# State-space input in one pass over the input blocks, values' projection in another PSUM bank, attention scores one tile earlier

## The chip, the cores and the metric

The kernel runs on one core of a Trainium2 chip. The core has a matrix engine (TensorE, PE in the profile, with its weight loads as PEld), VectorE (DVE), ScalarE (ACT), GpSimd (POOL) and SyncE (SP), which issues most DMAs. Matmul results go to PSUM: eight banks of 128 x 512 fp32. Everything else lies in SBUF. The metric is the device time of one execution in microseconds; the kernel before is given by the median of three runs.

## The reference

One decoder layer on 512 tokens of width 1024, all in fp32:

```
x = x + 1/2 SwiGLU(RMSNorm(x))
u = RMSNorm(x)
u_ssm, q, k, v, xq, g_ssm, g_attn, g_mem = split(u @ w_in)
branch 1: S5 state-space model on u_ssm (32 groups of 16 channels, 64 states each), GELU, GLU
branch 2: causal dilated attention, 3 patterns x 4 heads of 64, mixed by their softmax denominators
branch 3: cross attention (4 heads of 128) to 256 memory tokens
x = x + (sum over branches of sigmoid(gate) * branch) @ w_out
x = x + 1/2 SwiGLU(RMSNorm(x));  out = RMSNorm(x)
```

The output must agree with the fp32 reference, so almost every product is made of three fast matmuls: each operand is split into a rounded high part and the remainder (`wh`, `wl` for weights, `uh`, `ul` for the normalised input), and high x high, high x low and low x high are added up in PSUM.

## The kernel before

Activations stand transposed, as eight tiles of 128 features x 512 tokens. The input `u` of the middle part is held as `U`: eight pairs `uh[k]`, `ul[k]`. A weight chunk is 1024 x 256 (`load_chunk`, two buffers `wraw`); `split` (L120 to L126) makes its halves on ScalarE (L124) and VectorE (L125), three buffers each. `block_T` (L643) multiplies one 128-column half of a chunk with all of U: 8 blocks x 3 matmuls (L133, L134, L135) into one PSUM bank, 128 x 512.

In order of the program:

- Feed-forward 1 ends with the norm of x. `ffn1` (L632 to L638) then forms U block by block: VectorE makes `u` (L637), ScalarE `uh`, VectorE `ul` (L143, L144). While that goes on, TensorE works on keys and values of the memory tokens (`mem_kv`).
- The PSUM pool `ps_b` is opened for the middle part: two banks `mm` for projections, three `sc`, two `s1`, one `acc`.
- `ssm_in` (L652): four tiles of the state-space input, one after the other through `block_T` and the two `mm` banks. Each is copied to SBUF (`ub`, two buffers, L659) and written to a scratch in DRAM (`hd`, from ScalarE's queue, L661). `ssm_units` later reads it back in another layout (`stk`, on SP's queue, L676) and begins with matmuls into `s1` (L690).
- A loop over three chunks projects q, k and v. `split_q` and `split_k` (first chunk) copy a bank out in four and six pieces on ScalarE and VectorE (L930 to L942). `nat_rows` (L811) makes the values token by token: four row tiles of 128 x 256, two to a bank, 24 matmuls each (L822 to L824), again in the two `mm` banks. After each projection `tick` advances the state-space work.
- Cross attention, with its gates, uses `sc` and `s1`.
- Attention (L1003 to L1035): two pairs of heads x four row tiles, d = 0 to 7. `attn_tile` (L853) makes for two heads the scores (`sc` and `s1`: L862, L870), adds the bias and takes the maximum on VectorE (L874, L876), does the softmax (ScalarE L767, VectorE L769, L770), transposes the probabilities on TensorE (twelve, L883, through `sc` banks, copied out by ScalarE, L884) and multiplies with v into the bank `acc` (L890). After each tile come, for the same d, the state-space gate (24 matmuls) and the gated product of the state-space output (`pb`, `pa`, 12 matmuls each). After four tiles `acc` is split into `ath`, `atl`, the input of the attention's up-projection in the next stage.

The program's order is not the order on an engine. A planner takes each engine's instructions by priority, which follows the order of emission with a few shifts (`cur_priority`, `high_priority`), as soon as its own timing model calls them ready, and lays down a fixed order per engine. A tile of a pool gets its buffer or bank in that planning too. On the chip each engine then works strictly in its order and waits where an input or a buffer is late.

Of the kernel before, what the change touches and what calls it, by code (L numbers as in the profile page):

```python
# [20 lines left out]
P = 128  # L21
# [63 lines left out]
def kernel(ctx, tc, x, mem, ffn1_norm, ffn1_w_in, ffn1_w_down, mix_norm, w_in, a_re, a_im, log_dt,  # L85
# [21 lines left out]
    def load_chunk(w, k0, nk, c0, ncol):  # L107
        raw = wpool.tile([P, nk, ncol], F32, name="wraw", tag="wraw", bufs=2)
        nc.sync.dma_start(raw, w[k0 * P:(k0 + nk) * P, c0:c0 + ncol].rearrange("(k p) c -> p k c", p=P))
        return raw  # L110
# [532 lines left out]
    def block_T(raw, j):  # L643
        p = ps_tile("mm")
        mm_T(p, split(raw[:, :, j * P:(j + 1) * P]), U)
        return p
# [3 lines left out]


    def ssm_in(pool):  # L652
        hd = []
        for i in range(0, 4, 2):
            raw = load_chunk(W, 0, KD, i * P, 2 * P)
            for j in range(2):
                p = block_T(raw, j)
                b = pool.tile([P, T], F32, name="ub", tag="ub", bufs=2)
                S.activation(b, p, AF.Copy)  # L659
                d = dpool.tile([P, T], F32, name=f"hd{i + j}")  # L660
                nc.scalar.dma_start(d, b)  # L661
                hd.append(d)
        return hd

    def ssm_units(pool, hd):
# [93 lines left out]

    def softmax_rows(s, mx, pool, scale, n, tag, pr=None):  # L760

        nm = pool.tile([P, 1], F32, name=tag + "nm", tag=tag + "nm", bufs=2)
        V.tensor_scalar(nm, mx, -scale, None, op0=ALU.mult)
        sm = pool.tile([P, 1], F32, name=tag + "sm", tag=tag + "sm", bufs=2)
        if pr is None:
            pr = pool.tile([P, n], F32, name=tag + "p", tag=tag + "p", bufs=2)
        S.activation(pr, s, AF.Exp, bias=nm, scale=scale, accum_out=sm)  # L767
        ri = pool.tile([P, 1], F32, name=tag + "ri", tag=tag + "ri", bufs=2)
        V.reciprocal(ri, sm)  # L769
        V.tensor_scalar(pr, pr, ri, None, op0=ALU.mult)  # L770
        return pr
# [36 lines left out]
            for t in range(2):  # L808
                nc.scalar.dma_start(kvd[4 + 2 * t + c], mvs[t].rearrange("p a k -> p (a k)").bitcast(F32))

    def nat_rows(raw, src, nt, dst, eng=None):  # L811

        pss = [ps_tile("mm") for _ in range((nt + 1) // 2)]
        ws = [split(raw[:, kk:kk + 4, :], eng or V) for kk in range(0, KD, 4)]
        for t in range(nt):
            o = pss[t // 2][:, (t % 2) * 256:(t % 2) * 256 + 256]
            for k in range(KD):
                h, l = ws[k // 4]
                h, l = h[:, k % 4, :], l[:, k % 4, :]
                ah, al = src[k]  # L820
                ah, al = ah[:, t * P:(t + 1) * P], al[:, t * P:(t + 1) * P]
                TE.matmul(o, ah, h, start=k == 0, stop=False)  # L822
                TE.matmul(o, ah, l, start=False, stop=False)  # L823
                TE.matmul(o, al, h, start=False, stop=k == KD - 1)  # L824
        for t in range(nt):
            o = pss[t // 2][:, (t % 2) * 256:(t % 2) * 256 + 256]
            dst(t, o)
# [22 lines left out]
        return xo  # L850


    def attn_tile(pool, hp, r, qT, kT, v, bias, pacc):  # L853

        tok = slice(r * P, (r + 1) * P)
        pts = []
        heads = (2 * hp, 2 * hp + 1)
        s0 = [ps_tile("sc", 3) for _ in heads]
        s1 = [ps_tile("s1", 2) for _ in heads]
        kh, kl = kT[hp]  # L860
        for e in range(2):
            whole = TE.matmul(s0[e], qT[hp][e][:, tok], kh[e], start=True, stop=False)  # L862

        last = whole.ins
        rows = [(s0[e], qT[hp][e][halves[e], tok], kl[halves[e], :], False) for e in range(2)]
        rows += [(s1[e][:, p * P:(p + 1) * P], qT[2 * p + 2 + hp][halves[e], tok], kT[2 * p + 2 + hp][halves[e], tok], True)
                 for p in range(2) for e in range(2)]
        for o, q, k, st in rows:
            with tc.issue_after(last):
                last = TE.matmul(o, q, k, start=st, stop=True).ins  # L870
        for e, h in enumerate(heads):
            sb = pool.tile([P, 6 * P], F32, name="sb", tag="sb", bufs=3)
            mx = pool.tile([P, 2], F32, name="amx", tag="amx", bufs=3)
            V.tensor_tensor_reduce(sb[:, :T], s0[e], bias[h][:, (3 - r) * P:(7 - r) * P], scale=1.0, scalar=NEG,  # L874
                                   op0=ALU.add, op1=ALU.max, accum_out=mx[:, 0:1])
            V.tensor_tensor_reduce(sb[:, T:], s1[e][:, :256], bias[h][:, 7 * P:9 * P], scale=1.0, scalar=mx[:, 0:1],  # L876
                                   op0=ALU.add, op1=ALU.max, accum_out=mx[:, 1:2])
            pr = softmax_rows(sb, mx[:, 1:2], pool, 1.0, 6 * P, "at", pr=sb)
            pt = pool.tile([P, 6, P], F32, name="pt", tag="pt", bufs=4)
            for b0, nb in ((0, 4), (4, 2)):  # L880
                ta = ps_tile("sc", 3)
                for b in range(nb):
                    TE.transpose(ta[:, b * P:(b + 1) * P], pr[:, (b0 + b) * P:(b0 + b + 1) * P], ident)  # L883
                S.activation(pt[:, b0:b0 + nb, :], ta[:, :nb * P].rearrange("p (k q) -> p k q", k=nb), AF.Copy)  # L884
            pts.append(pt)

        for b in (4, 5, 0, 1, 2, 3):
            for e in (1, 0):
                kt, c = (b, heads[e] * 64) if b < 4 else (r, (b - 3) * 256 + heads[e] * 64)
                TE.matmul(pacc[halves[e], tok], v[kt][:, c:c + 64], pts[e][:, b, :], start=b == 4, stop=b == 3)  # L890

    def up_block(raw, j, src):
# [53 lines left out]
    for c in range(3):  # L946
        for lst, nm, base in ((qT, "q", 512), (kT, "k", 1280)):
            raw = load_chunk(W, 0, KD, base + c * 256, 256)
            for j in range(2):
                p = block_T(raw, j)  # L950
                if c == 0:
                    lst.append((split_q if nm == "q" else split_k)(p, j))
                else:
                    o = qp.tile([P, T], F32, name=f"{nm}T{2 * c + j}", tag=f"{nm}T{2 * c + j}")
                    S.activation(o, p, AF.Copy, scale=0.125 if nm == "q" else 1.0)
                    lst.append(o)
                tick()
        raw = load_chunk(W, 0, KD, 2048 + c * 256, 256)
        nat_rows(raw, U, 4, lambda t, o: V.tensor_copy(v[t][:, c * 256:(c + 1) * 256], o))
        tick()  # L960

    tick(1000)
# [40 lines left out]
    with sb_pool("att") as ap:  # L1003
        A, bias = [], []
        for h in range(4):
            bt = ap.tile([P, 9, P], F32, name=f"bias{h}")
            for g in range(4):
                src = bass.AP(tensor=brep.tensor, offset=brep.offset + h * 9 * 256 + 127 - 32 * g,
                              ap=[[NB - 1, 32], [256, 9], [1, P]])
                nc.sync.dma_start(bt[32 * g:32 * g + 32], src)  # L1010
            bias.append(bt.rearrange("p s k -> p (s k)"))
        for hp in range(2):
            pacc = ps_tile("acc", 1)
            for r in range(4):
                attn_tile(ap, hp, r, qT, kT, v, bias, pacc)
                d = 4 * hp + r
                if d not in gates:
                    ssm_gate(d)
                if d % 2 == 0:
                    rg = wpool.tile([P, 8, 2 * P], F32, name="wraw", tag="wraw", bufs=2)  # L1020
                    for s in range(2):
                        nc.sync.dma_start(rg[:, 4 * s:4 * s + 4, :],
                                          w_glu[0][:, s * D + d * P:s * D + (d + 2) * P].rearrange("(k p) c -> p k c", p=P))
                j = d % 2
                g = gates[d]
                pb = up_block(rg[:, 4:8, :], j, Y)
                t = gp.tile([P, T], F32, name="glt", tag="glt", bufs=2)
                S.activation(t, pb, AF.Tanh, scale=0.25)
                pa = up_block(rg[:, 0:4, :], j, Y)
                V.scalar_tensor_tensor(t, t, 1.0, pa, op0=ALU.add, op1=ALU.mult)  # L1030
                V.scalar_tensor_tensor(t, g, 1.0, t, op0=ALU.add, op1=ALU.mult)
                V.scalar_tensor_tensor(merged[d], t, 0.25, merged[d], op0=ALU.mult, op1=ALU.add)
            A.append((qp.tile([P, T], F32R, name=f"ath{hp}", tag=f"qs{hp}0"),
                      qp.tile([P, T], F32R, name=f"atl{hp}", tag=f"qs{hp}1")))
            split_plain(pacc, *A[-1])  # L1035
# [280 lines left out]
```

## Time and profile before

| | |
|---|---|
| Median of 3 runs | 1258.8 us (1258.47 to 1259.54) |
| The profiled execution | 1257.0 us, its span 1255.2 us |
| TensorE busy | 1232.7 us, 98% |
| VectorE, ScalarE, GpSimd busy | 793.4, 468.1, 102.6 us |
| Granted TensorE clock, mean | 0.997 |
| State-space input, first to last matmul | 413.4 to 438.5 us |
| First values' projection begins | 465.7 us |
| Attention, first transposes to last values | 686.0 to 798.2 us |

A row of the timeline gives start, duration, engine, line of the kernel, operation, output <- inputs, shape, count, and in brackets the idle time of the engine before it with what ended it. A row of the waits gives the waiting engine and line, what it waited for, us in total, times, longest. A row of the windows gives the stretch, its length, the busy time of each engine with its instructions, the granted clock, the DMA engines' share and GB/s (with a filter to one engine, only that one). A row of the groups gives line, engine, operation, tensors, shapes, count, busy us, mean ns, and idle time before with its releasers. Starts of matmuls overlap: one begins before its predecessor has drained, so the step from start to start is the rate.

### The profile page before, as it was taken

The numbers are of one execution on the slowest core, as the hardware profiler recorded it, in microseconds if no ns is written. First come the engines' busy times: TensorE is split into PE (matmuls) and PEld (weight loads), VectorE is DVE, ScalarE is ACT, GpSimd is POOL, SyncE is SP. The second block draws the span as 40 slices with busy tenths as digits, with TensorE's granted clock in tenths as the row PEclk, the third lists the DMA queues.
The fourth block names the chain that finished last, engine by engine and source line by source line (L and its number), as shares of the span: only waits on it lengthen the run. The fifth ranks groups of instructions, "written<-read, shape, count | busy, mean of one in ns | idle before, by whom it ended". The sixth has DMA issues, their size and how long they took to land.

```text
span 1255.2 us, 17065 instructions
## 1 busy us (share of the span) xinstructions
PE 1232.7 (98%) x6692; PEld 1046.6 (83%) x6692; DVE 793.4 (63%) x1514; ACT 468.1 (37%) x731; POOL 102.6 (8%) x83
## 2 busy tenths in 40 slices
PE   7999999999999999999999999899999999999997
PEld 6888888788889789998878777788888899899896
DVE  7999456876547567644535555455498557657664
ACT  4322232233324433234433444334245445345343
POOL 3000000000003033330000000001200001001002
PEclk9999999999999999999999999999999999999999
DMA  6233323754218844653118222234625457457411
GB/s 204 86 113 117 135 95 100 186 172 148 93 61 270 253 144 145 193 163 104 51 34 193 67 68 76 67 110 139 184 80 167 103 150 183 125 149 181 123 64 67
DMA packets 165767, 162.01 MB, mean 129 GB/s; under 512 B 28180, under 2 KB 149076, under 8 KB 165396
## 3 DMA queue, kind: packets, MB, share of 16 engines
q1 hardware_dynamic: 133488, 137.68, 35.1%
q0 software_dynamic: 8576, 8.65, 4.7%
q10 hardware_dynamic: 23624, 14.61, 3.9%
q8 instruction: 52, 0.85, 0.3%
q14 instruction: 27, 0.22, 0.1%
HBM read 145.94 MB, written 16.16 MB: 129 GB/s over the span
## 4 chain that ended last, share of the span: by engine, by line
PE 94%; DVE 3%; DMA 1%; ACT 1%; issue 0%; SPq 0%; ACTq 0%
PE ps_mm L133 21%; PE ps_mm L134 20%; PE ps_mm L135 20%; PE ps_mm L1160 4%; PE ps_mm L1161 4%; PE ps_mm L1158 4%; PE ps_mm L1216 3%; PE ps_mm L1217 3%; PE ps_mm L1218 3%; PE ps_mm L822 1%; PE ps_mm L824 1%; PE ps_mm L823 1%; PE ps_sc L883 1%; DMA wraw<-in_ffn_w_in_dram 1%; PE ps_sc L733 1%; PE ps_acc L890 1%
## 5 line engine op out<-in xcount | busy, mean ns | idle before, releaser
L124 ACT ACTIVATE wh<-wraw 128x1024 fp32r<-128x1024 f32 (+2 forms) x226 | 211.5, 938 | 470.3 <-PE ps_mm L134 330.5
L125 DVE TENSOR_TENSOR wl<-wraw,wh 128x1024 fp32r<-128x1024 f32 (+2 forms) x226 | 248.6, 1102 | 141.2 <-ACT wh L124 140.6
L133 PE MATMUL ps_mm<-uh,wh 128*128 128x512 f32 x768 | 301.8, 393 | 0.8 <-ACT uh L143 0.6
L134 PE MATMUL ps_mm<-ul,wh 128*128 128x512 f32 x768 | 300.4, 391 | 1.8 <-DVE ul L144 1.8
L135 PE MATMUL ps_mm<-uh,wl 128*128 128x512 f32 x768 | 299.9, 391 | 0.0
L134 PEld LDWEIGHTS ps_mm<-ul,wh 128*128 128x128 f32 x768 | 144.3, 188 | 32.8 <-DVE ul L144 2.8
L133 PEld LDWEIGHTS ps_mm<-uh,wh 128*128 128x128 f32 x768 | 144.3, 188 | 32.1 <-ACT uh L143 1.0
L135 PEld LDWEIGHTS ps_mm<-uh,wl 128*128 128x128 f32 x768 | 144.2, 188 | 29.9
L217 POOL TENSOR_TENSOR sqacc<-sqacc,sqk 128x512 f32<-128x512 f32 x12 | 20.2, 1682 | 686.1 <-ACT sqk L216 686.0
L134 PE MATMUL ps_mm<-gl,wh 128*128 128x512 f32 x176 | 70.0, 398 | 0.0
L133 PE MATMUL ps_mm<-gh,wh 128*128 128x512 f32 x176 | 69.9, 399 | 0.0
L135 PE MATMUL ps_mm<-gh,wl 128*128 128x512 f32 x176 | 69.8, 398 | 0.0
L1217 PE MATMUL ps_mm<-wl,gh 128*128 128x512 f32 x176 | 69.4, 394 | 0.0
L1218 PE MATMUL ps_mm<-wh,gl 128*128 128x512 f32 x176 | 69.1, 394 | 0.0
L1216 PE MATMUL ps_mm<-wh,gh 128*128 128x512 f32 x176 | 67.6, 395 | 0.0
L125 DVE TENSOR_TENSOR wl<-s,wh 128x1024 fp32r<-128x1024 f32 x32 | 39.2, 1224 | 42.8 <-ACT wh L124 42.8
L124 ACT ACTIVATE wh<-s 128x1024 fp32r<-128x1024 f32 x32 | 33.9, 1061 | 61.7 <-PE ps_mm L1218 26.1
L143 ACT ACTIVATE gh<-ff_t 128x512 fp32r<-128x512 f32 x44 | 27.1, 627 | 52.6 <-DVE ff_t L315 33.6
L135 PEld LDWEIGHTS ps_mm<-gh,wl 128*128 128x128 f32 x176 | 33.0, 188 | 8.2 <-issue 0.2
L133 PEld LDWEIGHTS ps_mm<-gh,wh 128*128 128x128 f32 x176 | 33.0, 188 | 8.2 <-issue 0.2
L1218 PEld LDWEIGHTS ps_mm<-wh,gl 128*128 128x128 f32 x176 | 33.2, 188 | 7.7
L1217 PEld LDWEIGHTS ps_mm<-wl,gh 128*128 128x128 f32 x176 | 33.2, 188 | 7.5
(395 smaller groups left out, 2388.8 us busy)
## 6 DMA issues: line engine op xcount, KB each, us to landing
wraw<-in_ffn_w_in_dram SPq DMA_DIRECT2D x34, 1024.0 KB, 5.2
wraw<-in_w_in_dram SPq DMA_DIRECT2D x25, 1024.0 KB, 5.4
wraw<-in_ffn_w_down_dram SPq DMA_DIRECT2D x12, 768.0 KB, 4.4
s<-in_ffn_w_in_dram SPq DMA_DIRECT2D x16, 512.0 KB, 3.7
s<-in_ffn_w_in_dram POOLq DMA_DIRECT2D x16, 512.0 KB, 6.2
wraw<-in_ffn_w_down_dram SPq DMA_DIRECT2D x8, 1024.0 KB, 5.2
wraw<-in_ffn_w_down_dram SPq DMA_DIRECT2D x10, 512.0 KB, 3.5
wraw<-in_xattn_w_kv_dram SPq DMA_DIRECT2D x4, 1024.0 KB, 8.0
```

The costliest lines, as they stand in the source:

```text
L124: S.activation(h, raw, AF.Copy)
L125: eng.tensor_tensor(l, raw, h.bitcast(F32), op=ALU.subtract)
L133: TE.matmul(ps, h[:, k, :], rhs[k][0], start=first and k == 0, stop=False)
L134: TE.matmul(ps, h[:, k, :], rhs[k][1], start=False, stop=False)
L135: TE.matmul(ps, l[:, k, :], rhs[k][0], start=False, stop=last and k == n - 1)
L143: S.activation(h, src, AF.Copy)
L1158: TE.matmul(o, h[:, k, cols], rhs[k][0], stop=False, **st)
L1160: TE.matmul(o, h[:, k, cols], rhs[k][1], stop=False, **st)
L1161: TE.matmul(o, l[:, k, cols], rhs[k][0], stop=k == 3, **st)
L1216: TE.matmul(pd[r], gh[:, tok], h, start=st, stop=False)
L1217: TE.matmul(pd[r], gh[:, tok], l, start=False, stop=False)
L1218: TE.matmul(pd[r], gl[:, tok], h, start=False, stop=en)
```

## The change

Three places are edited.

1. `ssm_in`: both weight chunks are loaded first, and four banks (two `mm`, two `s1`) are taken at once. For each block k of U the three matmuls of all four tiles are emitted, so the tiles grow together and end together. The weights are split by halves of k (blocks 0 to 3, then 4 to 7) over the whole 256 columns, instead of by column halves over all k. The copies and the writes of `hd` come after all matmuls.
2. `nat_rows` gets a flag `spare`, set for the values of the q, k, v loop: its first bank (tokens 0 to 255) is `acc`, its second `mm`.
3. `attn_tile` is cut into `attn_scores` (scores, bias, softmax) and `attn_values` (transposes, product with v). The scores of tile d + 1 are emitted before the values of tile d. The score tiles have four buffers instead of three, the small softmax columns four instead of two.

```diff
     def ssm_in(pool):
+        raws = [load_chunk(W, 0, KD, i * P, 2 * P) for i in (0, 2)]
+        ps4 = [ps_tile("mm"), ps_tile("mm"), ps_tile("s1", 2), ps_tile("s1", 2)]
+        for k0 in range(0, KD, 4):
+            hl = [split(raw[:, k0:k0 + 4, :]) for raw in raws]
+            for i in range(4):
+                uh_, ul_ = U[k0 + i]
+                for t in range(4):
+                    h, l = (z[:, i, (t % 2) * P:(t % 2 + 1) * P] for z in hl[t // 2])
+                    TE.matmul(ps4[t], h, uh_, start=k0 + i == 0, stop=False)
+                    TE.matmul(ps4[t], l, uh_, start=False, stop=False)
+                    TE.matmul(ps4[t], h, ul_, start=False, stop=k0 + i == KD - 1)
         hd = []
-        for i in range(0, 4, 2):
-            raw = load_chunk(W, 0, KD, i * P, 2 * P)
-            for j in range(2):
-                p = block_T(raw, j)
-                b = pool.tile([P, T], F32, name="ub", tag="ub", bufs=2)
-                S.activation(b, p, AF.Copy)
-                d = dpool.tile([P, T], F32, name=f"hd{i + j}")
-                nc.scalar.dma_start(d, b)
-                hd.append(d)
+        for t in range(4):
+            b = pool.tile([P, T], F32, name="ub", tag="ub", bufs=2)
+            S.activation(b, ps4[t], AF.Copy)
+            d = dpool.tile([P, T], F32, name=f"hd{t}")
+            nc.scalar.dma_start(d, b)
+            hd.append(d)
         return hd
...
-    def nat_rows(raw, src, nt, dst, eng=None):
-        pss = [ps_tile("mm") for _ in range((nt + 1) // 2)]
+    def nat_rows(raw, src, nt, dst, eng=None, spare=False):
+        pss = [ps_tile("acc", 1) if spare and i == 0 else ps_tile("mm") for i in range((nt + 1) // 2)]
...
-    def attn_tile(pool, hp, r, qT, kT, v, bias, pacc):
+    def attn_scores(pool, hp, r, qT, kT, bias):
...
-            sb = pool.tile([P, 6 * P], F32, name="sb", tag="sb", bufs=3)
+            sb = pool.tile([P, 6 * P], F32, name="sb", tag="sb", bufs=4)
...
-            pr = softmax_rows(sb, mx[:, 1:2], pool, 1.0, 6 * P, "at", pr=sb)
+            prs.append(softmax_rows(sb, mx[:, 1:2], pool, 1.0, 6 * P, "at", pr=sb))
+        return prs
+
+    def attn_values(pool, hp, r, prs, v, pacc):
+        tok = slice(r * P, (r + 1) * P)
+        pts = []
+        for pr in prs:
...
+        ahead = attn_scores(ap, 0, 0, qT, kT, bias)
         for hp in range(2):
             pacc = ps_tile("acc", 1)
             for r in range(4):
-                attn_tile(ap, hp, r, qT, kT, v, bias, pacc)
                 d = 4 * hp + r
+                prs, ahead = ahead, None
+                if d < 7:
+                    ahead = attn_scores(ap, (d + 1) // 4, (d + 1) % 4, qT, kT, bias)
+                attn_values(ap, hp, r, prs, v, pacc)
```

More of the change, by code (lines that the diff above doesn't have):

```diff
@@ L760, in softmax_rows @@
     def softmax_rows(s, mx, pool, scale, n, tag, pr=None):
-        nm = pool.tile([P, 1], F32, name=tag + "nm", tag=tag + "nm", bufs=2)
+        nm = pool.tile([P, 1], F32, name=tag + "nm", tag=tag + "nm", bufs=4)
         V.tensor_scalar(nm, mx, -scale, None, op0=ALU.mult)
-        sm = pool.tile([P, 1], F32, name=tag + "sm", tag=tag + "sm", bufs=2)
+        sm = pool.tile([P, 1], F32, name=tag + "sm", tag=tag + "sm", bufs=4)
         if pr is None:
@@ L767, in softmax_rows @@
         S.activation(pr, s, AF.Exp, bias=nm, scale=scale, accum_out=sm)
-        ri = pool.tile([P, 1], F32, name=tag + "ri", tag=tag + "ri", bufs=2)
+        ri = pool.tile([P, 1], F32, name=tag + "ri", tag=tag + "ri", bufs=4)
         V.reciprocal(ri, sm)
@@ L850, in xattn_head @@
         return xo
-    def attn_tile(pool, hp, r, qT, kT, v, bias, pacc):
+    def attn_scores(pool, hp, r, qT, kT, bias):
         tok = slice(r * P, (r + 1) * P)
-        pts = []
+        prs = []
         heads = (2 * hp, 2 * hp + 1)
@@ L871, in attn_tile @@
         for e, h in enumerate(heads):
-            sb = pool.tile([P, 6 * P], F32, name="sb", tag="sb", bufs=3)
-            mx = pool.tile([P, 2], F32, name="amx", tag="amx", bufs=3)
+            sb = pool.tile([P, 6 * P], F32, name="sb", tag="sb", bufs=4)
+            mx = pool.tile([P, 2], F32, name="amx", tag="amx", bufs=4)
             V.tensor_tensor_reduce(sb[:, :T], s0[e], bias[h][:, (3 - r) * P:(7 - r) * P], scale=1.0, scalar=NEG,
@@ L888, in attn_tile @@
             for e in (1, 0):
-                kt, c = (b, heads[e] * 64) if b < 4 else (r, (b - 3) * 256 + heads[e] * 64)
+                kt, c = (b, (2 * hp + e) * 64) if b < 4 else (r, (b - 3) * 256 + (2 * hp + e) * 64)
                 TE.matmul(pacc[halves[e], tok], v[kt][:, c:c + 64], pts[e][:, b, :], start=b == 4, stop=b == 3)
@@ L958 @@
         raw = load_chunk(W, 0, KD, 2048 + c * 256, 256)
-        nat_rows(raw, U, 4, lambda t, o: V.tensor_copy(v[t][:, c * 256:(c + 1) * 256], o))
+        nat_rows(raw, U, 4, lambda t, o: V.tensor_copy(v[t][:, c * 256:(c + 1) * 256], o), spare=True)
         tick()
```

## The prediction

> **What bounds the kernel now.** I read the page's busy shares, then TensorE's waits, then the timeline at each of the three edited places.
>
> ```profile
> span 1255.2 us, 17065 instructions
> PE 1232.7 (98%) x6692; PEld 1046.6 (83%) x6692; DVE 793.4 (63%) x1514; ACT 468.1 (37%) x731; POOL 102.6 (8%) x83
> PE 94%; DVE 3%; DMA 1%; ACT 1%; issue 0%; SPq 0%; ACTq 0%
> ...
> PE ps_sc L883 <- DVE sb L770: 2.4, 1, 2.4
> ...
> PE ps_mm L134 <- DVE ul L144: 1.8, 2, 1.6
> PE ps_mm L822 <- DVE kl L942: 1.3, 1, 1.3
> PE ps_mm L133 <- ACT ath L143: 0.7, 1, 0.7
> PE ps_mm L133 <- ACT uh L143: 0.6, 1, 0.6
> PE ps_acc L890 <- ACT pt L884: 0.5, 1, 0.5
> ```
>
> TensorE is the bound: 98% of the span, 94% of the chain. No edit changes the number of matmuls, so time can only come from its waits. The six shown sum to 7.3 us, and each belongs to one of the edited places: U's late blocks (L134 and L133 on ul, uh), the values' projection (L822 on kl), the last attention tile (L883, L890, L133 on ath). Waits understate the loss, because TensorE also runs slowly beside them. So I compare each place with its own undisturbed rate.
>
> **Part 1, state-space input.** Beside the stage stand its undisturbed end and what VectorE does meanwhile.
>
> ```profile
> 413.44 0.40 PE L133 MATMUL ps_mm<-uh,wh 128*128 128x512 f32 x1
> ...
> 425.62 0.39 PE L133 MATMUL ps_mm<-uh,wh 128*128 128x512 f32 x1
> ...
> 438.31 0.39 PE L135 MATMUL ps_mm<-uh,wl 128*128 128x512 f32 x1
> 438.54 0.38 PE L690 MATMUL ps_s<-stk,blhs 128*128 128x128 f32 x2
> ...
> 425.60:438.50 12.90, 12.90 (x58) 1.00 0.75 216
> ...
> 415.90:423.00 7.10, 4.77 (x18) 2.92 (x18) 6.67 (x11) 2.91 (x5) 0.14 (x2) 1.00 0.97 295
> ...
> 418.84 0.42 DVE L144 TENSOR_TENSOR mvs<-ps_mm,mvs 128x256 fp32r<-128x256 f32 x1
> ...
> 421.23 1.47 DVE L144 TENSOR_TENSOR ul<-u,uh 128x512 fp32r<-128x512 f32 x2
> 424.38 1.23 DVE L125 TENSOR_TENSOR wl<-wraw,wh 128x1024 fp32r<-128x1024 f32 x1 [1.68 <-ACT wh L124]
> ...
> 414.22 1.06 ACT L124 ACTIVATE wh<-wraw 128x1024 fp32r<-128x1024 f32 x1 [0.41 <-DMA wraw<-in_w_in_dram]
> ```
>
> The stage has 4 tiles x 8 blocks x 3 = 96 matmuls, from 413.44 to 438.54: 25.10 us. From 425.62 to 438.31 they run freely: the window holds 58, one begun before it, so 57 starts and 56 steps, 12.69 / 56 = 0.227 us. 96 of them take 21.8 us; **3.3 us are lost**, because VectorE, full from 415.9 to 423.0, delivers the last blocks of U only at 422.7, while one tile eats a block in 3 x 0.227 = 0.7 us.
>
> After the change one block feeds 12 matmuls, 2.7 us. Block 4 is wanted at 413.44 + 4 x 2.72 = 424.3, after all eight exist. The splits stay four of 128x1024, the evictions and the writes of hd four each, so nothing is added. What is new is demand. The second chunk's first half is wanted after six matmuls, at 414.8; its ScalarE half can begin at 414.22, where it waited for its load, so with 1.06 + 1.2 it is there at 416.5. If the planner's order goes strictly through the tiles, TensorE waits 1.7 us; if it runs the first two tiles ahead (18 matmuls with U's blocks 0 to 2, 4.1 us, are ready), nothing. The last half-split needs the first one's buffer (three in all), free after 42 matmuls at 413.44 + 9.5 = 423.0, ready 2.3 later at 425.3, wanted after 54 at 425.7: 0.4 to spare. Finally the four tiles now take four banks at once, and the memory values leave one bank only at 419.26; should a tile fall on it, its first matmul, otherwise at 413.44 + 9 x 0.227 = 415.5, waits up to 3.8 us. Bounds: 0 to 3.8 lost again. I take 0.4: the present order already interleaves tiles, and three unblocked ones hold 36 matmuls, 8.2 us.
>
> ```profile
> hd<-ub ACTq DMA_DIRECT2D x4, 256.0 KB, 3.8
> stk<-hd SPq DMA_DIRECT2D x12, 64.0 KB, 2.2
> ```
>
> The moved DMAs: all four tiles end within nine matmuls (2.0 us) at 435.2 instead of 5.4 us apart, so the first write of hd leaves ScalarE's queue near 433.2 + 0.6 = 433.8, and stk lands near 433.8 + 3.8 + 2.2 = 439.8. The third eviction waits there for that write (two buffers ub); behind it on ScalarE stand the splits of the coming q and k tiles and q's evictions, the first wanted when q's first tile ends at 440.7. On SP the stk loads wait for the same write, and the next weight loads queue behind them; those chunks are wanted only after four tiles. Unit 0's matmuls (L690) come after q's second tile in program order, at 435.2 + 2 x 5.44 = 446. Slack 6 us: cost 0, bounds 0 to the rival below.
>
> A rule of the Trainium skill speaks against the new loop: TensorE: Matmul & The Clock Gate, section "A second HAM failure mode: psum-queue depth-cycling", tells of a kernel that cycled through PSUM banks each iteration and fell back and forth between full and half clock. Its result is a rival below.
>
> **Part 2, values' projection.**
>
> ```profile
> 464.03 0.39 PE L135 MATMUL ps_mm<-uh,wl 128*128 128x512 f32 x1
> 465.69 0.36 PE L822 MATMUL ps_mm<-wh,uh 128*128 128x256 f32 x1 [1.27 <-DVE kl L942]
> ...
> 471.40 0.28 PE L824 MATMUL ps_mm<-wh,ul 128*128 128x256 f32 x1
> ...
> 464.85 0.69 DVE L942 TENSOR_TENSOR kl<-ps_mm,kh 64x512 fp32r<-64x512 f32 x1 [1.27 <-ACT kh L941]
> 465.79 1.75 DVE L125 TENSOR_TENSOR wl<-wraw,wh 128x1024 fp32r<-128x1024 f32 x1 [0.25 <-ACT wh L124]
> ```
>
> The next matmul was due at 464.03 + 0.23 = 464.26 and came at 465.69: **1.43 us lost** to k's eviction holding the bank. The acc bank is idle until attention, so tokens 0 to 255 begin at once; their 48 matmuls, 465.69 to 471.40 here and so 0.12 us each, last 5.8, past the bank's release at 465.5, which the other half then takes. What is late next is the weights' second half-split, 467.54: after 24 matmuls, at 467.1. I give back 0.3 (bounds 0 to 0.9, the latter when k's second tile holds ScalarE longer). The second and third projections show no wait and gain nothing.
>
> **Part 3, attention.** The timeline of the last tile, and TensorE's clock in it:
>
> ```profile
> 786.04 1.72 PE L883 MATMUL ps_sc<-ident,sb 128*128 128x128 f32 x12
> 787.60 0.99 PE L862 MATMUL ps_sc<-kh,qs 128*128 128x512 f32 x2
> ...
> 789.39 1.53 PE L890 MATMUL ps_acc<-pt,v 128*64 128x128 f32 x24
> 793.36 2.80 PE L883 MATMUL ps_sc<-ident,sb 128*128 128x128 f32 x12 [2.44 <-DVE sb L770]
> 796.69 1.53 PE L890 MATMUL ps_acc<-pt,v 128*64 128x128 f32 x24 [0.53 <-ACT pt L884]
> ...
> 799.41 0.50 PE L133 MATMUL ps_mm<-uh,wh 128*128 128x512 f32 x1
> ...
> 793.00:797.00 4.00, 3.10 (x18) 2.73 (x20) 1.00 (x3) 2.03 (x6) 0.00 (x0) 0.57 0.00 0
> ```
>
> Tile 7's scores come last of all (787.60), when the gates and the gated product of tile 7 and even the next stage's first gate are used up. Nothing covers its softmax, and after the 2.44 us of idling the granted clock from 793 to 797 is 0.57 in the mean: a half rate for (1 - 0.57) x 4 / 0.5 = 3.4 us of it. Undisturbed, from 789.39: values 1.53, transposes 787.60 - 786.04 = 1.56, values 1.53, one up-projection matmul 0.23, so the stream would resume at 794.2. It resumes at 799.41: **5.2 us lost**. With scores(7) ahead of transposes(6), at least tile 6's 48 gate and product matmuls lie between scores(7) and transposes(7): 48 x 0.23 = 11 us over a chain that took 793.36 - 789.39 = 4.0 at its shortest. Tile 7's own 48 then cover A's split.
>
> Each tile moves 2 + 2 + 4 score matmuls, four VectorE reductions and two exponentials ahead of the preceding tile's transposes and their evictions. Of three score banks two are then held until VectorE has read them.
>
> ```profile
> L874 DVE CUSTOM_DVE_ANT_0 sb<-ps_sc,bias 128x512 f32<-128x512 f32 x15 | 9.8, 687 | 6.5 <-PE ps_sc L870 6.2 <-DMA bias<-brep 0.3
> ...
> L884 ACT ACTIVATE pt<-ps_sc 128x512 f32<-128x512 f32 x16 | 9.6, 598 | 13.8 <-PE ps_sc L883 13.8
> ```
>
> Transposes(d) have four groups for one free bank: the worst is two reductions and two evictions exposed, 2 x 0.69 + 2 x 0.60 = 2.6 us per tile, seven tiles. The cover is the 11 us of gate and product matmuls; I charge 0.6 in all (bounds 0 to 18).
>
> **Sum.** 3.3 + 1.4 + 5.2 = 9.9 recoverable; give back 0.4 + 0.3 + 0.6 = 1.3: 8.6 us. The profiled execution took 1257.0 (span 1255.2 and 1.8 around it), so 1248.4; the median of the runs shown, 1258.8, is 1.8 above it: **1250.2 us**.
>
> **Rivals.**
>
> *One gain of the three does not come.* TensorE's order is written by a planner from priorities and its own timings, so emission need not become order, and U's four banks may collide as above. Without part 1: 1250.2 + 2.9 = 1253.1; without part 3: 1250.2 + 4.6 = 1254.8. For it: each wait seen has a planner's order behind it. Against: the waits' causes (VectorE's rate, a held bank, a last tile) are what is edited.
>
> *The round trip of hd becomes the wait.* Already now the first L690 stands directly behind the stage, at 438.54. If it does again, at 435.2, TensorE waits until 439.8, 4.6 us, and some 1.7 more at half clock (the 3.4 us above): 1250.2 + 6.3 = 1256.5. Against: then its data had long landed; a planner that prices DMAs puts it later.
>
> *Slower: transposes starve of score banks.* It decides above 9.9 / 7 = 1.4 us per tile; at the full 2.6 it costs 18 us, 1258.8 - 9.9 + 18 = 1267. For it: two of three banks taken. Against: the filler, and that the present order already runs scores(d+1) before values(d).
>
> *Bank cycling halves the clock.* At half rate the stage takes 2 x 21.8 = 43.6 instead of the 22.2 forecast: 1250.2 + 21.4 = 1271.6. Rows of this kernel where gate and up-projection alternate banks at each step stand against it:
>
> ```profile
> 803.62 0.39 PE L133 MATMUL ps_mm<-uh,wh 128*128 128x512 f32 x1
> 803.85 0.40 PE L134 MATMUL ps_mm<-atl,wh 128*128 128x512 f32 x1
> 804.09 0.39 PE L135 MATMUL ps_mm<-ath,wl 128*128 128x512 f32 x1
> 804.32 0.39 PE L134 MATMUL ps_mm<-ul,wh 128*128 128x512 f32 x1
> ```
>
> They start 0.23, 0.24, 0.23 apart: no idling at a change of bank. By the Trainium skill's rule the half clock would show here; the trace disagrees.
>
> **How the numbers follow.** Forecast 0.60; one gain missing 0.18; hd's round trip 0.07; neither gain nor loss, several give-backs together, 0.05; starved transposes 0.08; bank cycling 0.02. A measurement of this kernel tells 0.2%, 2.5 us, from no change. Faster: 0.60 + 0.18 + half of hd's (1256.5 is near the edge, 1256.3) = 0.81; same 0.09; slower 0.10. The range begins where all 9.9 come, at 1258.8 - 9.9 = 1248.9, less the spread of the runs (1258.47 to 1259.54, 1.1) and an estimate of 0.8 for what a reordered stream may close besides (half of the 1.3 given back), 1247.0, and ends at 1257.0, taking in the missing gain and hd's round trip; starvation and cycling stay outside.
>
> **What would show it.** Right: no wait of L133 or L134 on uh or ul and the 96 matmuls in about 22 us; L822 directly behind L135 in the first projection; transposes of the last tile without a wait on sb, and the granted clock 1.00 through attention. Wrong: waits of L883 on pt (L884) or sb in each tile, of L690 on stk, of ps_s on the memory values; or the last tile's scores still behind the gates of the next stage.

## The result and the profile after

The changed kernel takes 1250.83 us (median of 4 runs, 1250.67 to 1251.07), the kernel before beside it 1258.63 us (4 runs, 1257.6 to 1259.54). The ratio is 0.9935, with an interval of 0.992 to 0.995: faster by 7.8 us. The forecast was 1250.2. The profiled execution took 1250.94 us.

The page of the changed kernel, its head and its chain of waits in shares:

```profile
span 1249.2 us, 17053 instructions
...
PE 1231.3 (99%) x6692; PEld 1046.2 (84%) x6692; DVE 793.7 (64%) x1514; ACT 466.8 (37%) x731; POOL 101.6 (8%) x83
...
PE 94%; DMA 2%; DVE 2%; ACT 1%; issue 0%; SPq 0%; ACTq 0%; DVEq 0%
```

TensorE runs the same 6692 matmuls. Of the 6.0 us that the span lost, 4.6 were idle time (22.5 us before, 17.9 after); the other 1.4 lie in its busy time, 1232.7 before and 1231.3 after, where slow stretches count as busy. What TensorE waits for now (total, times, longest, in us):

```profile
PE ps_tr L255 <- DMA g_in<-in_ffn_norm_dram: 2.2, 1, 2.2
PE ps_mm L274 <- ACT wh L124: 2.1, 1, 2.1
PE ps_tr L263 <- DMA xn<-in_x_dram: 1.9, 1, 1.9
PE ps_s L663 <- DVE wl L125: 1.0, 1, 1.0
PE ps_mm L133 <- ACT wh L124: 0.9, 1, 0.9
PE ps_tr L223 <- DVE sqacc L217: 0.6, 1, 0.6
PE ps_s L662 <- ACT wh L124: 0.4, 1, 0.4
PE ps_mm L133 <- DVE ff_a L310: 0.3, 1, 0.3
```

All the waits that the prediction listed are gone: on ul and uh, kl, sb, pt and ath. The three near 2 us lie at the kernel's start and are there before too. New are two in the state-space input (L662 on wh, L663 on wl, 1.4 us together), one of 0.9 us (L133 on wh) and one of 0.6 us (L223). The last lies at 395.8 us, ahead of every edited place, and a second profile of the same changed kernel does not have it, so it is not the edit's.

The timeline of the changed kernel at the three edited places, TensorE, and two rows of VectorE and ScalarE:

```profile
414.87 0.39 PE L662 MATMUL ps_mm<-uh,wh 128*128 128x512 f32 x1
...
416.03 0.39 PE L664 MATMUL ps_mm<-ul,wh 128*128 128x512 f32 x1
...
416.80 0.50 PE L662 MATMUL ps_s<-uh,wh 128*128 128x512 f32 x1 [0.38 <-ACT wh L124]
...
418.33 0.50 PE L663 MATMUL ps_s<-uh,wl 128*128 128x512 f32 x1 [1.03 <-DVE wl L125]
...
423.66 0.39 PE L662 MATMUL ps_s<-uh,wh 128*128 128x512 f32 x1
...
424.34 0.39 PE L662 MATMUL ps_s<-uh,wh 128*128 128x512 f32 x1
...
425.02 0.39 PE L662 MATMUL ps_mm<-uh,wh 128*128 128x512 f32 x1
...
438.62 0.39 PE L133 MATMUL ps_mm<-uh,wh 128*128 128x512 f32 x1
...
456.59 0.39 PE L135 MATMUL ps_mm<-uh,wl 128*128 128x512 f32 x1
456.82 0.28 PE L831 MATMUL ps_acc<-wh,uh 128*128 128x256 f32 x1
...
772.53 0.93 PE L898 MATMUL ps_sc<-ident,sb 128*128 128x128 f32 x7
...
778.61 1.53 PE L905 MATMUL ps_acc<-pt,v 128*64 128x128 f32 x24
...
415.69 1.06 ACT L124 ACTIVATE wh<-wraw 128x1024 fp32r<-128x1024 f32 x1 [0.74 <-DMA wraw<-in_w_in_dram]
...
417.06 2.35 DVE L125 TENSOR_TENSOR wl<-wraw,wh 128x1024 fp32r<-128x1024 f32 x2
```

In the state-space input the third tile (in the bank ps_s) is reached after six matmuls. Its weights' first half waits 0.74 us on ScalarE for its load, then VectorE makes the low part from 417.06 (two such halves in its row), and TensorE stands behind it until 418.33. From there it runs freely, through all four banks in turn: three matmuls take 0.68 us. The values' first projection starts directly behind k's last matmul, in the attention's bank. The last tile's transposes and values carry no wait; the values end near 780, where they ended near 798 before.

The stages, each from the first matmul of one mark to the first of the next, in us of the profiled executions:

```text
                                              before   after    difference
up to the state-space input                   413.44   414.87     +1.43
state-space input                              25.24    23.75     -1.49
q, k and values, up to the cross attention    130.28   128.88     -1.40
cross attention to feed-forward 2 (last L223) 329.56   325.01     -4.55
the rest                                      356.66   356.66      0.00
span                                         1255.18  1249.17     -6.01
```

The 0.9 us on L133 lie in the fourth row. The +1.43 is not the edit's: 0.95 of it is there already at feed-forward 1's first matmul (36.38 before, 37.33 after), in code that is the same, and the wait on L223 is large enough for the rest; a later profile of the same changed kernel (in "Again on one chip" below) reaches the state-space input at 413.11.

### The profile page after: what moved, and what is told of

Same layout as the page of the kernel before. It is cut to its first block, busy times and chain, and to the rows that moved or that the text cites. A ratio compares the mean times of both kernels' runs of the same rounds, so it can differ in the third digit from the quotient of the medians.

```text
span 1249.2 us, 17053 instructions
## 1 busy us (share of the span) xinstructions
PE 1231.3 (99%) x6692; PEld 1046.2 (84%) x6692; DVE 793.7 (64%) x1514; ACT 466.8 (37%) x731; POOL 101.6 (8%) x83
## 4 chain that ended last, share of the span: by engine, by line
PE 94%; DMA 2%; DVE 2%; ACT 1%; issue 0%; SPq 0%; ACTq 0%; DVEq 0%
PE ps_mm L133 20%; PE ps_mm L134 20%; PE ps_mm L135 20%; PE ps_mm L1179 4%; PE ps_mm L1180 4%; PE ps_mm L1177 4%; PE ps_mm L1235 3%; PE ps_mm L1237 3%; PE ps_mm L1236 3%; PE ps_acc L905 1%; PE ps_sc L898 1%; PE ps_sc L742 1%; DMA wraw<-in_ffn_w_in_dram 1%; DMA wraw<-in_xattn_w_kv_dram 1%; DVE wl L125 1%; PE ps_mm L833 1%
## 5 line engine op out<-in xcount | busy, mean ns | idle before, releaser
L133 PE MATMUL ps_mm<-uh,wh 128*128 128x512 f32 x736 | 288.9, 393 | 1.2 <-ACT wh L124 0.9
L135 PE MATMUL ps_mm<-uh,wl 128*128 128x512 f32 x736 | 287.9, 391 | 0.0
L134 PE MATMUL ps_mm<-ul,wh 128*128 128x512 f32 x736 | 287.6, 391 | 0.0
L133 PEld LDWEIGHTS ps_mm<-uh,wh 128*128 128x128 f32 x736 | 138.3, 188 | 30.1 <-issue 1.7
L135 PEld LDWEIGHTS ps_mm<-uh,wl 128*128 128x128 f32 x736 | 138.2, 188 | 28.7 <-issue 0.2
L134 PEld LDWEIGHTS ps_mm<-ul,wh 128*128 128x128 f32 x736 | 138.3, 188 | 28.5 <-issue 0.2
L133 PE MATMUL ps_mm<-gh,wh 128*128 128x512 f32 x176 | 69.9, 399 | 0.0
L124 ACT ACTIVATE wh<-s 128x1024 fp32r<-128x1024 f32 x32 | 33.9, 1061 | 61.4 <-PE ps_mm L1237 26.1
L133 PEld LDWEIGHTS ps_mm<-gh,wh 128*128 128x128 f32 x176 | 33.0, 188 | 8.2 <-issue 0.2
```

Source lines behind the costliest of these rows:

```text
L124: S.activation(h, raw, AF.Copy)
L133: TE.matmul(ps, h[:, k, :], rhs[k][0], start=first and k == 0, stop=False)
L134: TE.matmul(ps, h[:, k, :], rhs[k][1], start=False, stop=False)
L135: TE.matmul(ps, l[:, k, :], rhs[k][0], start=False, stop=last and k == n - 1)
```

## The experiments

Every edit is against the kernel before unless it says "changed kernel" or "pairs first". Medians of the kernel before are of the same chip: 1258.32 us for the first four, 1259.64 for "Ahead from tile 5 on" and "Again on one chip", 1258.85 for the other four.

**Part 1 alone.** The new ssm_in, nothing else.

```diff
 def ssm_in(pool):
...
+        for k0 in range(0, KD, 4):
+            hl = [split(raw[:, k0:k0 + 4, :]) for raw in raws]
+            for i in range(4):
...
+                for t in range(4):
...
-        for i in range(0, 4, 2):
-            raw = load_chunk(W, 0, KD, i * P, 2 * P)
-            for j in range(2):
-                p = block_T(raw, j)
...
```

> Only the state-space input's four tiles grow together; values' projection and attention as before. Theory (each edit closes its own stall, and the strict order over the tiles gives back what the profile after shows, waits of 0.38 and 1.03 us in front of the second chunk's tiles): the stage shrinks from 25.1 to about 23.7 us, the kernel gains 1.3 to 1.5 us, and the wait of L822 on kl (1.3 us) and the end of attention (2.4 us on sb) stay. Rival (the whole 3.3 us come and were eaten by something else in the changed kernel): 2.8 us or more.

1257.07 us (1255.0 to 1258.69, 12 runs), ratio 0.9986, 0.9975 to 0.9996: 1.3 us less. The interval reaches from 0.5 to 3.1 us, so the times alone do not exclude the rival; the stage does, with 23.82 us instead of 25.24. TensorE's waits in it, and the window of the last attention tile (the last columns before the DMA's share are the granted clock):

```profile
PE ps_sc L892 <- DVE sb L779: 2.4, 1, 2.4
...
PE ps_s L663 <- DVE wl L125: 1.2, 1, 1.2
PE ps_mm L831 <- DVE kl L951: 1.2, 1, 1.2
...
PE ps_s L662 <- ACT wh L124: 0.2, 1, 0.2
```

```profile
788.00:803.00 15.00, 11.17 (x87) 8.78 (x88) 4.89 (x17) 5.82 (x11) 0.00 (x0) 1.00 0.03 10
```

The two new waits in the stage come with this edit alone, and the old ones on kl and sb stay. In this execution the 2.4 us of idling in attention did not lower the clock, which stays 1.00.

**Part 2 alone.** The first bank of the values' projection from the attention's tag.

```diff
-        pss = [ps_tile("mm") for _ in range((nt + 1) // 2)]
+        pss = [ps_tile("acc", 1) if spare and i == 0 else ps_tile("mm") for i in range((nt + 1) // 2)]
```

> Only the values' projection takes the acc bank first. Theory (the held bank was the whole cause): gain 1.1 to 1.5 us, the wait of L822 on kl gone, nothing new in its place. Rival (the next late thing is the weights' second half-split, or k's second tile): gain 0.3 to 0.8 us with a wait of L823 on wl.

1259.82 us (1257.47 to 1266.92, 12 runs), ratio 1.0015, 0.9998 to 1.0032: no gain, where the theory had 1.1 to 1.5 us. Its waits, and the granted clock at the two old idle places:

```profile
PE ps_mm L1161 <- DVE wl L125: 1.5, 1, 1.5
...
PE ps_mm L133 <- ACT wh L124: 0.9, 1, 0.9
```

```profile
417.00:424.00 7.00, 4.93 (x15) 3.66 (x15) 6.23 (x10) 2.79 (x5) 0.14 (x2) 0.76 0.99 334
...
793.00:798.00 5.00, 4.03 (x32) 3.42 (x34) 1.03 (x3) 2.04 (x6) 0.00 (x0) 0.69 0.00 0
```

The wait on kl is gone, and from q to the cross attention its profile takes 128.79 us, 1.49 less than before. But a wait of 0.9 us stands at the first block of feed-forward 2, 430 us later, in code that the edit doesn't touch, and one of 1.5 us inside feed-forward 2. The first is in the changed kernel too. The second varies: the same line waits 0.2 us in part 1 alone and 0.3 in one of the two profiles of pairs first, and not in the other; its cause stays open. This execution also ran at a lowered clock at both old idle places. So this run shows no gain, but its 1.5 us above the kernel before are neither clear of noise nor shown to be the edit's, and the three parts run alone (1.3, -1.5 and 5.8 us) do not add up to the 7.8 of the whole.

**Part 3 alone.** Scores one tile ahead.

```diff
-                attn_tile(ap, hp, r, qT, kT, v, bias, pacc)
+                prs, ahead = ahead, None
+                if d < 7:
+                    ahead = attn_scores(ap, (d + 1) // 4, (d + 1) % 4, qT, kT, bias)
+                attn_values(ap, hp, r, prs, v, pacc)
```

> Only the attention's scores are emitted one tile ahead. Theory (the last tile's uncovered softmax and the half clock behind it are the price): gain 4.4 to 5.2 us, no wait of L883 on sb, granted clock 1.00 throughout attention. Rival (part of the gain in the changed kernel comes from the earlier start of attention after parts 1 and 2): gain under 4 us.

1252.48 us (1252.18 to 1253.33, 5 runs), ratio 0.9946, 0.9929 to 0.9963: 5.8 us less, somewhat more than expected. From the cross attention to feed-forward 2 the profile takes 323.89 us instead of 329.56, which is 5.67 less, 0.9 of it a half clock that only the profile before has there (part 1 alone, without it, takes 328.66). No wait on sb, pt or ath is left, and none of transposes on a score bank has come. Part 3 also brings a fourth score buffer and four softmax columns instead of two; these alone were not run, here or in the two partial versions below, which keep them.

**Pairs first.** The changed kernel; within each half of the input blocks, the first chunk's two tiles take their four blocks before the second chunk's tiles begin.

```diff
-            for i in range(4):
-                for t in range(4):
+            for i, t in [(i, t) for t2 in (0, 2) for i in range(4) for t in (t2, t2 + 1)]:
```

> The changed kernel, but within each half of U's blocks the first chunk's two tiles take all four blocks before the second chunk's two tiles begin. Theory (the strict order made TensorE wait for the second chunk's load and split, while 24 matmuls of the first chunk were ready): the two waits, 1.4 us, and the slow steps beside them go, the stage comes to 21.8 to 22.2 us, the kernel to about 1249.0. Rival (U's blocks 1 to 3 are then wanted twice as fast, one every 1.4 us, and VectorE delivers them late): new waits on uh or ul of the same size, time as the changed kernel, 1250.8.

1248.88 us (1248.66 to 1250.79, 5 runs), ratio 0.9921, 0.9902 to 0.994. The timeline of its state-space input:

```profile
414.76 0.40 PE L661 MATMUL ps_mm<-uh,wh 128*128 128x512 f32 x1
...
420.02 0.39 PE L663 MATMUL ps_mm<-ul,wh 128*128 128x512 f32 x1
420.25 0.39 PE L661 MATMUL ps_s<-uh,wh 128*128 128x512 f32 x1
```

The third tile now begins 5.5 us into the stage, when its weights are split, and no wait is left: 21.81 us instead of 23.75. So the 1.4 us of waits in the changed kernel's stage, and 0.5 us beside them, come from the strict order over four tiles.

**The last tile alone ahead.** Tile 7's scores stand ahead of tile 6's transposes; all others as before.

```diff
+                if prs is None:
+                    prs = attn_scores(ap, hp, r, qT, kT, bias)
+                if d == 6:
+                    ahead = attn_scores(ap, 1, 3, qT, kT, bias)
+                attn_values(ap, hp, r, prs, v, pacc)
```

> The kernel before with one difference: only the last attention tile's scores are emitted one tile ahead; the first seven tiles, the state-space input and the values' projection stay as before. Theory (all that the third edit gains is the cover of the last tile's softmax): time of the third edit alone, 1252.5 within 0.6 us, clock 1.00 in attention. Rival (running ahead in every tile closes something in the steady part too, by steadier order): clearly above, 1254 or more.

1256.06 us (1254.36 to 1257.72, 11 runs), ratio 0.9978, 0.9969 to 0.9987: 2.8 us, half of what all tiles ahead give, so the theory fails and its rival holds. The timeline of its attention's end:

```profile
784.67 0.73 PE L862 MATMUL ps_sc<-kh,qs 128*128 128x512 f32 x2
...
794.11 0.87 PE L889 MATMUL ps_sc<-ident,sb 128*128 128x128 f32 x6
795.73 1.53 PE L896 MATMUL ps_acc<-pt,v 128*64 128x128 f32 x24 [0.74 <-ACT pt L890]
...
797.95 0.50 PE L133 MATMUL ps_mm<-ath,wh 128*128 128x512 f32 x1 [0.70 <-ACT ath L143]
```

The wait on sb is gone, as meant, but the waits on pt and ath stand. Counted from the start of the cross attention (568.96 us before, 570.86 here), the last values end after 226.4 us instead of 229.3; in part 3 alone it is 212.7. With only this tile moved, the gates and products are still used up before its values.

**Ahead from tile 5 on.** The same with tiles 5, 6 and 7 (`if 3 < d < 7`).

> The kernel before with the scores one tile ahead only from tile 5 on (emitted in tiles 4, 5 and 6); the rest as before. With the last tile alone ahead 2.8 us came, with all tiles 5.8. Theory (the planner lets gates and products run ahead of the attention tiles, so that by the last tile the cover is spent; each tile that runs ahead keeps some of it back): time between the two, 1253 to 1255, last values near 785 to 790 us, less waiting behind them. Rival (three tiles are enough to bring the last values in front of the remaining matmuls): as with all tiles, 1252.5. Second rival (the gain lies in the first tiles): as with the last alone, 1256.

1255.53 us (1253.62 to 1256.2, 9 runs), ratio 0.9965, 0.9952 to 0.9978: 4.1 us, between the two as the theory has it, though 0.5 us above its range. Its last values begin at 795.53, not near 785 to 790, and end 225.2 us after the start of the cross attention; the wait on pt is gone, that on ath remains. From the cross attention to feed-forward 2 the profiles take 328.66 us (none ahead: part 1 alone, whose clock is whole there), 326.74 (the last), 325.48 (three) and 323.89 (all). In these profiles each step is worth 1.3 to 1.9 us; the intervals of the times of the neighbouring steps overlap.

**Kept busy.** The kernel before, with ten more 128x512 matmuls behind tile 7's scores whose result nothing uses.

```diff
+        if hp == 1 and r == 3:
+            keep_busy = ps_tile("sc", 3)
+            for _ in range(10):
+                with tc.issue_after(last):
+                    last = TE.matmul(keep_busy, qT[hp][0][:, tok], kh[0], start=True, stop=True).ins
```

> The kernel before, with ten added matmuls of 128x512 (2.3 us) whose result nobody uses, in the idle time in front of the last tile's transposes. Theory (part of the price of that idle time is a half clock that comes in some executions and not in others, and that makes the kernel's times scatter over some 7 us): the transposes start where they did, always at full clock, the median falls by 1 to 2 us to about 1257 and the scatter to that of the kernels without the idle time, 1 to 2 us. Rival (the scatter comes from elsewhere, the half clock is cheap): median within 0.5 us of 1258.3 and times still 5 us or more apart.

1258.22 us (1257.04 to 1259.37, 11 runs), ratio 0.9994, 0.9985 to 1.0003: nothing that can be told from no change in the median, where the theory had 1 to 2 us. The runs lie 2.3 us apart where those of the kernel before beside them lie 4.9 us apart (1256.99 to 1261.85, 21 runs); neither the theory's scatter nor the rival's came. TensorE's rows at the place, and the granted clock further up, at the state-space input's old stall:

```profile
793.98 2.59 PE L875 MATMUL ps_sc<-kh,qs 128*128 128x512 f32 x10
...
796.41 1.84 PE L888 MATMUL ps_sc<-ident,sb 128*128 128x128 f32 x12
```

```profile
418.00:420.00 2.00, 0.99 (x4) 0.25 (x2) 2.00 (x4) 0.83 (x2) 0.00 (x0) 1.00 0.90 236
420.00:422.00 2.00, 0.92 (x4) 0.79 (x5) 2.00 (x5) 0.82 (x2) 0.00 (x0) 1.00 1.07 363
422.00:424.00 2.00, 2.00 (x7) 1.57 (x6) 1.97 (x4) 1.18 (x2) 0.14 (x2) 0.58 0.98 303
424.00:426.00 2.00, 2.00 (x7) 1.52 (x6) 0.70 (x2) 0.08 (x1) 0.00 (x0) 0.56 0.97 307
```

The ten matmuls fill the idle place, and the twelve transposes behind them take 1.84 us where they took 2.80 before. The stretch from the cross attention to feed-forward 2 takes 328.75 us, like part 1 alone (328.66) and 0.8 less than the kernel before. In this execution the half clock came at the other idle place, where the state-space input takes 26.26 us instead of 25.24. So idling at either place can lower the clock, and filling one leaves the other.

**Without part 2.** Pairs first, with the values' projection as before.

> The version with the first chunk's two tiles running ahead, but values' projection in the two mm banks as before. Theory (the second edit gains 1.4 us at the first values' projection and pays 0.9 us for a split that the planner then lays down late at the start of feed-forward 2, since that wait stands in the three profiles with this edit and in none of the three without): the wait of L822 on kl returns with 1.3 us, the wait of L133 on wh (0.9 us, near 885) goes, the time is 0.4 to 0.6 us above 1248.9. Rival (the late wait is not the second edit's): 1.4 us above, 1250.3, with both waits.

1249.12 us (1248.24 to 1249.89, 5 runs), ratio 0.9921, 0.9908 to 0.9934. Its timeline at the first projection:

```profile
463.17 0.35 PE L830 MATMUL ps_mm<-wh,uh 128*128 128x256 f32 x1 [1.25 <-DVE kl L956]
```

The wait on kl is back, 1.25 us, and the 0.9 us at feed-forward 2 is gone. From the cross attention to feed-forward 2 it takes 323.93 us where pairs first takes 325.01, so part 2's wait costs 1.1 us there and part 2 is left with 0.3 to 0.4 of its 1.4 to 1.5. By the medians it is worth about 0.2 us, which can't be told from nothing.

**The spare bank in the first projection only.** Pairs first, with the attention's bank used by the first of the values' projections alone.

```diff
-        nat_rows(raw, U, 4, lambda t, o: V.tensor_copy(v[t][:, c * 256:(c + 1) * 256], o), spare=True)
+        nat_rows(raw, U, 4, lambda t, o: V.tensor_copy(v[t][:, c * 256:(c + 1) * 256], o), spare=c == 0)
```

> The version with the first chunk's two tiles running ahead, with the acc bank only in the first values' projection, where the wait was. Theory (the late split at the start of feed-forward 2 comes from how the planner's buffers fall out, not from a resource): the time moves by 0 to 0.9 us down from 1248.9, without the wait on wh if the buffers fall out otherwise. Rival (the second and third projections gain from the bank too): 0.5 us or more above.

1248.75 us (1247.85 to 1249.56, 5 runs), ratio 0.9919, 0.9904 to 0.9934. The 0.9 us at feed-forward 2 is still there; which bank or buffer passes it on stays open.

**Again on one chip.** The changed kernel and pairs first, side by side.

> The changed kernel itself, on the same chip and against the same runs as the next one. Theory: 1250.8 within 0.5 us.

> The changed kernel with the first chunk's two tiles running ahead. Theory (what the strict order gave back is 1.9 us): 1248.9 within 0.6 us, its interval apart from that of the changed kernel. Rival (chips differ by as much): overlapping.

1251.19 us (1249.29 to 1251.88, 6 runs), ratio 0.9928, 0.9911 to 0.9946, and 1248.74 us (1247.83 to 1250.53, 6 runs), ratio 0.9912, 0.9893 to 0.9932. The intervals against the kernel before overlap, against the expectation, but five of the changed kernel's six runs lie above all six of pairs first, the medians differ by 2.45 us, and the stage takes 23.82 and 21.77 us in these profiles, as in the first pair. Pairs first is the best version run, faster by 0.8 to 0.9% than the kernel before; with part 2, without it or with it once it can't be told apart (1248.74 to 1249.12 us).

## Why the prediction was right, and where it was not

**The bound and the sum.** That TensorE bounds the kernel, and that time comes from its waits and the slow stretches beside them, held. The sum came out close, 8.6 us forecast and 7.8 measured, but partly by luck: of the three parts two came out smaller than forecast and one larger.

**Part 1** has the right mechanism and the wrong size: 1.3 to 1.5 us in place of 2.9. The waits on U's blocks are gone, as reckoned. The step that failed is "I take 0.4: the present order already interleaves tiles". The planner took the four tiles strictly in turn, and the other branch of that same step came true: it gave 1.7 us for the strict order, and 1.4 us of waits are seen (0.38 + 1.03), in a stage of 23.75 us against the free 21.8. Pairs first confirms the cause, for it changes the order alone and gets 1.9 us of the stage back. The order within an edited stage should have been counted with its worst branch, since no row of the profile said which the planner would take. The collision with the memory values' bank did not occur: the third and fourth tile waited for weights, not for a bank.

**Part 2** was worth 1.4 us locally (the stage from q to the cross attention shrank by 1.40 and, alone, 1.49), a little over the 1.1 forecast; the weights' second half-split that was to be late next isn't in the list of waits. What failed is that the sum ended there. A wait of 0.9 us, which costs 1.1 us of the stretch, appears at the start of feed-forward 2, where the weights' split is late:

```profile
886.27 0.47 PE L133 MATMUL ps_mm<-uh,wh 128*128 128x512 f32 x1 [0.88 <-ACT wh L124]
```

It comes and goes with part 2 (there in part 2 alone, in the changed kernel and in pairs first, with the spare bank once too; not in the kernel before nor in any version without part 2), so it belongs to that edit. That a buffer handed on by the planner's order carries it there is argued, not shown.

**Part 3** came to 5.8 us instead of 4.6. Its give-back of 0.6 wasn't paid: no transposes wait for a score bank. But its reason was too narrow. I laid the whole loss on the last tile's uncovered softmax; moving that tile alone brings 2.8 us. The waits that go add up to 3.9 us in the kernel before: 2.4 on sb, 0.5 on pt, 0.7 on ath, and 0.3 more at the end of the cross attention, which the prediction did not count. In part 3 alone a score matmul of tile 1 stands in its place (the second row):

```profile
657.94 0.50 PE L133 MATMUL ps_mm<-xoh,wh 128*128 128x512 f32 x1 [0.33 <-DVE mg L1000]
...
658.38 0.39 PE L862 MATMUL ps_sc<-kh,qs 128*128 128x512 f32 x1
```

Of these the last tile alone removes the 2.4 on sb; pt goes with three tiles ahead, ath and the 0.3 only with all. That gates and products are then left over for the end fits where the last values lie, 212.7 us after the start of the cross attention instead of 229.3. A half clock as in the profile before accounts for about 0.9 more: part 1 alone has these waits at full clock (pt 0.7 instead of 0.5) and takes 328.66 us over this stretch instead of 329.56. That leaves some 0.9 of the 5.67 us (5.67 - 3.9 - 0.9). Part of it is slow steps behind the waits: the first matmul on ath, at 798.92 before, is followed only at 799.41, 0.49 us where the free step is 0.23.

**The rivals.** Bank cycling fell: the three-matmul groups at 423.66, 424.34 and 425.02 start 0.68 us apart, 0.227 us a matmul as before, and the granted clock is 1.00 from the stage's start to its end:

```profile
414.80:438.60 23.80, 22.39 (x98) 18.02 (x98) 11.60 (x16) 8.98 (x14) 0.14 (x2) 1.00 0.69 228
```

What the Trainium skill tells (TensorE: Matmul & The Clock Gate, section "A second HAM failure mode: psum-queue depth-cycling") of a kernel whose matrix engine idles shortly between its groups of matmuls did not come in this loop, which cycles through banks too but waits nowhere behind 418.33. The round trip of hd fell: TensorE takes q's first tile first and comes to the state-space units without a wait, as the timeline and the view of the DMA queues show:

```profile
444.52 0.38 PE L699 MATMUL ps_s<-stk,blhs 128*128 128x128 f32 x2
...
449.77 1.72 PE L699 MATMUL ps_s<-stk,blhs 128*128 128x128 f32 x14
```

```profile
hd<-ub ACTq DMA_DIRECT2D x4, 256.0 KB, 2.0
...
stk<-hd SPq DMA_DIRECT2D x9, 64.0 KB, 2.3
```

The first write of hd leaves at 433.78, as forecast, and both DMAs together take 4.3 us. Unit 0's four loads of stk leave SP's queue between 435.83 and 437.57; with 2.3 us to landing they are there some 4.6 us before the units' first matmuls at 444.52, where the slack was reckoned at 6. Starved transposes fell, and the attention's clock stayed whole, in the changed kernel's windows against 0.57 in the prediction's:

```profile
680.00:780.00 100.00, 100.00 (x655) 79.84 (x654) 56.21 (x145) 46.33 (x93) 0.00 (x0) 1.00 0.25 72
780.00:800.00 20.00, 20.00 (x91) 16.27 (x88) 9.43 (x13) 6.67 (x12) 0.00 (x0) 1.00 0.28 92
```

The rival that one gain of three does not come came half true, for most of part 2's and half of part 1's, and part 3's surplus hid it in the sum.

## What to carry to other kernels

Where one change takes away several waits, run each part alone: here a total within 10% of its forecast was made of one part at half its size, one near nothing and one a quarter above. And take each part out of the whole too: part 2 alone looked like a loss in noisy runs, and only leaving it out showed its small gain and its price. In a loop that serves several tiles from weights that arrive in two loads, let the tiles of the first load go on until the second is split; the tight interleaving cost 1.9 us of the gain, and one line brought it back. And work that can cover a chain late in a stage must be saved for it by the tiles before: moving only the last chain forward gave about half.

## What was not expected of the hardware

An idle TensorE of 1.6 to 2.4 us lowers the granted clock in some executions and not in others. After 2.44 us on sb the clock was 0.57 over 4 us in the profile before and stayed 1.00 in part 1 alone; the stall on U's blocks in the state-space input was followed by the half clock in the profile of kept busy (rows above) and not in the profile before. Over all profiles with the place as it was, the clock fell in two of three after the idling in attention (before and part 2 alone, not part 1 alone) and in three of six at the stall in the state-space input (part 2 alone, ahead from tile 5 on, kept busy). A half-clock stretch cost about 0.9 us in the attention and 0.9 to 1.0 in the state-space input, which takes 26.1 to 26.3 us in the three profiles with it and 25.2 in the three without. The Trainium skill warns of such drops for "No PE-idle gaps >~3µs between matmul bursts" (TensorE: Matmul & The Clock Gate, section "Why this matters for your kernels"); the trace shows one after shorter gaps, but not reliably.

With the idle places the runs also seem to scatter more, though the numbers of runs differ. The kernel before ran from 1256.38 to 1263.45 us on the first chip (23 runs) and part 2 alone up to 1266.92, while part 3 alone stayed within 1.2 us (5 runs), pairs first within 2.1 (5) and 2.7 (6), and the changed kernel beside it within 2.6 (6). The slowest execution of the kernel before had a mean granted clock of 0.993, the fastest 0.998; by an estimate from the difference, 0.005 x 1257 = 6.3 us of full clock were lost. The half-clock stretch of 3.4 us in the profile before lost 1.7 us of full clock and cost 0.9, and at that rate the 6.3 make some 3.3 of the 7.1 us of scatter: the clock explains a good part, not shown to be all. Where in those executions the lost clock lies is open, as none of them was profiled.
